# Hybrid mixer block on one core: the 31-tap convolution moved to the tensor engine and behind attention, projection weights split one block ahead

## The chip, the cores and the metric

One core of one Trainium2 chip runs the whole kernel. The metric is the time of one execution in microseconds of the device. TensorE (PE) multiplies matrices, VectorE (DVE), ScalarE (ACT) and GpSimd (POOL) work element by element, SyncE (SP) issues nearly all transfers. Each engine works off one queue in order.

## The reference

The model has two layers over 1024 latent tokens of width 1024 and 256 context tokens (`TL`, `TC`). A layer projects the normalised tokens once (`p = h @ w_in[l]`) and gives slices of `p` to four mixers of 256 channels each; a second projection and a mixture of 32 experts follow. The second layer has no outputs for the context, so most of its projections take the latent tokens alone. The mixers:

```python
y_a = rglru_mixer(...)       # 4-tap convolution u, gates r and i from u (64x64 blocks), linear scan, both directions, gated by gelu
y_b = diff_attn_mixer(...)   # differential attention
y_c = conformer_conv(...)    # below
y_d = hyena_mixer(...)       # 3-tap convolution, then twice: long convolution by Fourier transforms, times a gate

def conformer_conv(pc, conv_w, conv_b, ln_g, ln_b, w_pw, b_pw):
    u = pc[..., :W_C] * jax.nn.sigmoid(pc[..., W_C:])
    u = dwconv(u, conv_w, conv_b, (CONF_K // 2, CONF_K // 2))   # 31 taps, each channel for itself
    u = layer_norm(u, ln_g, ln_b)
    return jax.nn.silu(u) @ w_pw + b_pw
```

All of it is float32. The kernel keeps products exact to about that by splitting operands into a high and a low half of a reduced type (`fp32r`) and multiplying three times.

## The kernel before

Channels lie on the partitions, tokens along them, in pieces (`GROUPS`) of 512, 512 and 256 (context). The source is written in stages, and a scheduler orders each engine's queue when the program is built: what stands earlier in the source goes first where its inputs are expected to be ready. A buffer (`bufs`) that is still read holds up the next writer.

*Projections* (`phase1`, L2050). `win` (L1052) computes blocks of 128 columns of `w_in`. For every block it loads the weights (`wir`, one buffer), rounds them to `wih` on ScalarE and subtracts to `wil` on GpSimd (L959; two buffers each); then each piece takes 24 matmuls (L1073) into one PSUM bank and an evacuation. Block 0 and 1 feed the recurrence, 2 and 3 its output gates, 4 to 7 queries and keys, 10 to 13 the convolution mixer's GLU (12, 13 are the sigmoid halves), 14 to 19 hyena. `win_v` (L1101, matmuls L1115) makes the values. The order written is: block 0, recurrence 0, GLU blocks 12 and 10, GLU blocks 13 and 11, gate block 2, block 1, recurrence 1, then queries, keys and values, gate block 3.

`rglru` (L1385) goes through three steps of two directions: `rg_u` (4 taps: one GpSimd instruction L1410 and three on VectorE L1412, one buffer), two gate matmuls (L1415, into three PSUM banks `rg` shared by all), ScalarE functions to `rg_r`, `rg_i`, `rg_t` (two buffers each, released by the scan), products on GpSimd and VectorE and the scan (L1432, L1435).

`glu_evac` (L1119) leaves the GLU's output in `cu` in SBUF. `conv31` (L1452) is written behind all projections: 31 VectorE instructions for each of two channel blocks, each over all tokens at once,

```python
for j in range(1, 31):
    nc.vector.scalar_tensor_tensor(a, u[:, j:j + N], cw(j), a, op0=OP.mult, op1=OP.add)   # L1459
nc.sync.dma_start(self.cd[b * P:(b + 1) * P, :N], a)
```

*Attention* (L1161) follows, with the hyena blocks 14 to 19 of `win` between its matmuls (`rest`, L2113). In layer 0 it also has one part of the modulation for layer 1 (`modulation`, L962; matmuls L987 of two columns into four groups of 32 PSUM partitions), whose weights are loaded into the buffers `xa` and `cu` of the projections.

*Mixer stage* (L2183 to 2205). The order written is: `hyena_in` (L1721: load `hx`, three taps `hu` on GpSimd L1735 and VectorE L1738, transposes L1745) for blocks 0 and 1, hyena's first forward transform (`next(hy)`; matmuls L1782 with tables `tabc`), attention's output to channels, `hyena_in` for blocks 2 to 5, the whole `conformer` (L1472: load of `cd`, layer norm, pointwise product for every piece), the split of the output weights, and the rest of hyena. The output projection follows.

## Time and profile before

| | |
|---|---|
| median of three timed runs | 3564.89 us (3561.86 to 3567.80) |
| the profiled execution | 3568.25 us, of which the span of the trace is 3566.4 us |
| mean granted TensorE clock | 0.925 |
| TensorE busy | 3093.1 us (87%) |
| VectorE busy | 2296.5 us (64%) |
| ScalarE busy | 1538.4 us (43%) |
| GpSimd busy | 712.2 us (20%) |
| transfers | 743.33 MB, 208 GB/s on the mean |

Rows are read as follows. "L1459 DVE ... cacc<-cu,cw,cacc 128x1295 x120" is a group of 120 VectorE instructions of line 1459 that write `cacc`; behind the bar stand busy time in all, mean nanoseconds of one, and the idle time of the engine just before them with what ended it. In rows of a timeline the start comes first, then the duration, then the instruction; "x8" means eight instructions merged. PEclk is the clock that TensorE was granted as a share of full speed. A float32 matmul leaves two records, an `fp32r` one a single record. The recorded length of a matmul includes its run through the array, so its pace is read from the starts of neighbours.

### The profile page before, as it was taken

To read this page: it belongs to the slowest core of one execution; us is meant where nothing else is said; L and a number is where in the kernel's file an instruction comes from. 1 tells how busy PE (TensorE), PEld (TensorE's weight loads), DVE (VectorE), ACT (ScalarE), POOL (GpSimd) and SP (SyncE) were. 2 spreads that over 40 slices of the span, in tenths; PEclk is the share of its full clock that TensorE was granted. 3 is DMA by queue.
4 is the path that set the end of the run, shared out by engine and by line. 5 is a ranking of instruction groups with operands and counts; after the bars stand their busy time and mean duration, and the time that the engine had idled before them with its cause. 6 is when DMAs were issued, how large, how long until landed. Compare 5 with 4: busy or idle time off the path is not lost. (4 is left out here: it accounts for less than half of the span.)

```text
span 3566.4 us, 43889 instructions
## 1 busy us (share of the span) xinstructions
PE 3093.1 (87%) x14984; PEld 2083.0 (58%) x14984; DVE 2296.5 (64%) x3355; ACT 1538.4 (43%) x2497; POOL 712.2 (20%) x573
## 2 busy tenths in 40 slices
PE   5798788997899699999998587799788799899996
PEld 1246665775678354677555466667667665455563
DVE  6675885787768434476544779578876764357645
ACT  4234334772324233465543454367433343245523
POOL 2213451003210101111110445300330111111100
PEclk8899989998999699999999698889989899999998
DMA  5752226215455889987878512312446389978797
GB/s 184 232 193 62 72 88 213 72 38 191 159 194 189 269 305 321 360 312 240 316 252 324 198 33 101 135 34 70 160 150 217 135 297 369 386 278 282 263 348 297
DMA packets 415375, 743.33 MB, mean 208 GB/s; under 512 B 46219, under 2 KB 181240, under 8 KB 415146
## 3 DMA queue, kind: packets, MB, share of 16 engines
q1 hardware_dynamic: 397546, 702.69, 56.9%
q0 software_dynamic: 17600, 37.79, 3.1%
q8 instruction: 119, 1.95, 0.2%
q14 instruction: 110, 0.90, 0.1%
HBM read 656.13 MB, written 105.30 MB: 214 GB/s over the span
## 5 line engine op out<-in xcount | busy, mean ns | idle before, releaser
L679 DVE TENSOR_TENSOR wl<-wr,wh 128x1024 fp32r<-128x1024 f32 (+1 forms) x440 | 515.7, 1202 | 341.7 <-ACT wh L678 334.4
L678 ACT ACTIVATE wh<-wr 128x1024 fp32r<-128x1024 f32 (+1 forms) x440 | 442.5, 1038 | 381.8 <-PE mm L730 229.7
L734 PE MATMUL mm<-wr,xl 128*64 128x512 f32 x1216 | 327.9, 609 | 4.4 <-DVE xl L690 1.6
L1073 PE MATMUL mm<-hh,wih 128*128 128x512 f32 (+1 forms) x752 | 289.7, 386 | 12.1 <-ACT stg L1137 7.0
L1073 PE MATMUL mm<-hh,wil 128*128 128x512 f32 (+1 forms) x752 | 288.0, 384 | 10.7 <-POOL wil L959 9.9
L730 PE MATMUL mm<-wh,xh 128*128 128x512 f32 x704 | 289.5, 413 | 6.2 <-ACT wh L678 5.7
L1073 PE MATMUL mm<-hl,wih 128*128 128x512 f32 (+1 forms) x752 | 289.7, 385 | 1.4 <-DVE hl L959 0.8
L730 PE MATMUL mm<-wl,xh 128*128 128x512 f32 x704 | 278.7, 396 | 5.2 <-DVE wl L679 5.2
L730 PE MATMUL mm<-wh,xl 128*128 128x512 f32 x704 | 277.9, 396 | 0.0
L798 POOL DMA_INDIRECT fd<-ot,ridx x82 | 103.1, 1258 | 851.2 <-DVE ot L794 392.7
L1459 DVE SCALAR_TENSOR_TENSOR cacc<-cu,cw,cacc 128x1295 f32<-128x1295 f32 (+1 forms) x120 | 193.9, 1616 | 1.9
L671 POOL DMA_INDIRECT gb<-h2d,ridx x82 | 98.4, 1200 | 449.4 <-PE tr L698 197.1
L730 PEld LDWEIGHTS mm<-wh,xh 128*128 128x128 f32 x704 | 134.0, 190 | 92.0 <-issue 47.5
L1207 DVE TENSOR_REDUCE m<-A 128x1 f32<-128x1024 f32 x128 | 156.2, 1220 | 44.1 <-PE A L1197 36.1
L959 POOL TENSOR_TENSOR wil<-wir,wih 128x1024 fp32r<-128x1024 f32 x34 | 93.2, 2742 | 429.6 <-ACT wih L956 374.2
L734 PEld LDWEIGHTS mm<-wr,xl 128*64 128x64 f32 x1216 | 96.4, 137 | 140.8 <-issue 123.6
L1073 PEld LDWEIGHTS mm<-hh,wih 128*128 128x128 f32 x752 | 146.8, 196 | 42.5 <-ACT stg L1137 10.6
L1073 PEld LDWEIGHTS mm<-hh,wil 128*128 128x128 f32 x752 | 146.8, 195 | 39.2 <-POOL wil L959 11.5
L1073 PEld LDWEIGHTS mm<-hl,wih 128*128 128x128 f32 x752 | 147.0, 196 | 30.6 <-issue 6.3
L780 PE MATMUL mm<-wr,hl 128*64 128x512 f32 x608 | 154.6, 602 | 0.0
L730 PEld LDWEIGHTS mm<-wl,xh 128*128 128x128 f32 x704 | 134.1, 191 | 33.3 <-DVE wl L679 9.2
L1252 ACT ACTIVATE wT<-TR 128x512 f32<-128x512 f32 (+1 forms) x200 | 104.7, 524 | 108.3 <-PE TR L1247 99.0
(492 smaller groups left out, 6536.8 us busy)
## 6 DMA issues: line engine op xcount, KB each, us to landing
wr<-in_moe_w_gate_dram SPq DMA_DIRECT2D x256, 512.0 KB
wr<-in_moe_w_up_dram SPq DMA_DIRECT2D x256, 512.0 KB
wr<-in_moe_w_down_dram SPq DMA_DIRECT2D x256, 512.0 KB
wada<-in_w_ada_dram SPq DMA_DIRECT2D x48, 512.0 KB
tabc<-in_k_t_c_dram SPq DMA_DIRECT2D x88, 256.0 KB
wir<-in_w_in_dram SPq DMA_DIRECT2D x40, 512.0 KB
wr<-in_w_ada_dram SPq DMA_DIRECT2D x32, 512.0 KB
ks<-qkd SPq DMA_DIRECT2D x16, 640.0 KB
```

The source lines that it names most:

```text
L671: self.K.nc.gpsimd.indirect_dma_start(out=g[s, :D // (1 + h)], out_offset=None, in_=self.h2d[h], in_offset=bass.IndirectOffsetOnAxis(ap=id ...
L678: nc.scalar.activation(hi, src, AF.Copy)
L679: nc.vector.tensor_tensor(lo, src, hi.bitcast(FT), op=OP.subtract)
L730: nc.tensor.matmul(ps[b][w], x(k), y[:, kk], start=(k == 0 and c == 0), stop=(k == 7 and c == 2))
L734: nc.tensor.matmul(ps[b][0][w * 64:(w + 1) * 64], self.XT[n0 + b](k), raw[w][:, kk], start=(k == 0), stop=(k == 7))
L780: nc.tensor.matmul(po[b][0][o * 64:(o + 1) * 64], HT[b][:, k], raw[:, o], start=(k == 0), stop=(k == 3))
L798: s = nc.gpsimd.indirect_dma_start(out=self.fd[h], out_offset=bass.IndirectOffsetOnAxis(ap=ridx[r], axis=0), in_=ot[r], in_offset=None, bo ...
L959: (eng or nc.vector).tensor_tensor(lo, src, hi.bitcast(FT), op=OP.subtract)
L1073: nc.tensor.matmul(p[:, :n], a[:, k], b[:, k, t0:t0 + n], start=(k == 0 and a is wh and b is hh), stop=(k == 7 and a is wl))
L1207: nc.vector.tensor_reduce(m[:, c, 1:2], A[c], axis=AX.X, op=OP.max, negate=True)
L1252: nc.scalar.activation(o, i_, AF.Copy)
L1459: nc.vector.scalar_tensor_tensor(a, u[:, j:j + N], cw(j), a, op0=OP.mult, op1=OP.add)
```

## The change

The 31-tap convolution leaves VectorE. `glu_evac` writes the GLU's output to DRAM (`ud`). In the mixer stage `taps` arranges the weights as 64 diagonal matrices of 32 columns (`tapw`: channel in the columns, four taps times 32 channels along the rows), and `conv31` loads each piece of `ud` four times, shifted by one token each (`cr4`), so that one matmul does four taps of 32 channels; eight steps and four groups of 32 channels make a piece of 128 channels. `conformer` becomes a generator whose products and norms are called between hyena's steps; `hyena_in` for blocks 4 and 5 moves behind hyena's first inverse transform. In the projections, `rglru_conv` computes the six pieces of `rg_u` ahead of the GLU blocks (six buffers), the gate blocks move between queries and keys, `win` prepares the weights of the next block (`nxt`) with the low half on VectorE, and `stg` gets a third buffer. The modulation in layer 0's attention gets buffers of its own. The leftover experts, which run only under a condition read at run time, get a factor in layer 1.

```diff
+        self.ud = self.dram.tile([2 * P, UW], FT, name="ud")
+        z = c.tile([P, 2, 16], FT, name="zeros")
+        nc.vector.memset(z, 0.0)
+        for o, n in ((0, 15), (15 + TL, 15), (30 + T0, 16)):
+            nc.sync.dma_start(self.ud[:, o:o + n].rearrange("(b p) t -> p b t", p=P), z[:, :, :n])
...
+    def win_weights(self, l, w, ob, eng=None):
+        nc = self.nc
+        wl = w.tile([P, 8, P], FR, name="wil", bufs=2)
+        raw = w.tile([P, 8, P], FT, name="wir", bufs=1)
+        nc.sync.dma_start(raw, self.I["w_in"][l, :, ob * P:(ob + 1) * P].rearrange("(k p) f -> p k f", p=P))
+        wh = w.tile([P, 8, P], FR, name="wih", bufs=2)
+        self.split(raw, wh, wl, eng=eng or nc.gpsimd)
+        return wh, wl
...
+        W = [self.ready.pop(ob, None) or self.win_weights(l, w, ob, eng) for ob in obs]
+        if nxt is not None and len(obs) == 1:
+            self.ready[nxt] = self.win_weights(l, w, nxt, nc.vector)
...
+                if nxt is not None and nxt not in self.ready and t0 == groups[-1][0] and len(obs) == 2:
+                    self.ready[nxt] = self.win_weights(l, w, nxt, nc.vector)
                 evac(p, t0, n, v)
...
         def g(p, t0, n, v):
             o = t0 + 15 + (15 if v else 0)
-            nc.vector.scalar_tensor_tensor(u[:, o:o + n], th[0][:, :n], 1.0, p[:, :n], op0=OP.add, op1=OP.mult)
+            t = th[0][:, :n]
+            nc.vector.scalar_tensor_tensor(t, t, 1.0, p[:, :n], op0=OP.add, op1=OP.mult)
+            nc.sync.dma_start(self.ud[b * P:(b + 1) * P, o:o + n], t)
...
+    def rglru_conv(self, l, w, b, xa):
+        nc, res = self.nc, []
+        for s in range(3):
+            for d in range(2):
...
+                u = w.tile([P, 512], FT, name="rg_u", bufs=6)[:, :n]
+                nc.gpsimd.tensor_scalar(u, xa[:, o:o + n], cw(0), self.pc("a_conv_b", d * 2 + b), op0=OP.mult,
+                                        op1=OP.add)
+                for j in range(1, 4):
+                    nc.vector.scalar_tensor_tensor(u, xa[:, o + j:o + j + n], cw(j), u, op0=OP.mult, op1=OP.add)
+                res.append(u)
...
+    def taps(self, l, w):
+        R = w.tile([64, 4, 32], FT, name="taps", bufs=1)
+        nc.gpsimd.memset(R, 0.0)
+        for j in range(8):
+            m = min(4, 31 - 4 * j)
+            nc.sync.dma_start(R[j * 8:(j + 1) * 8, :m],
+                              bass.AP(tensor=cw.tensor, offset=cw.offset + 4 * j * 256, ap=[[32, 8], [256, m], [1, 32]]))
+        p = self.pr.tile([P, 512], FT, name="rg")
+        nc.tensor.transpose(p[:, :64], R.rearrange("r s c -> r (s c)"), self.ident[:64, :64])
+        t = w.tile([P, 64], FT, name="tapsT", bufs=1)
+        nc.scalar.activation(t, p[:, :64], AF.Copy, scale=0.5)
...
+        W = w.tile([P, 64, 32], FT, name="tapw", bufs=1)
+        nc.gpsimd.tensor_tensor(W, one[:, None, :].to_broadcast([P, 64, 32]), t[:, :, None].to_broadcast([P, 64, 32]),
+                                op=OP.mult)
...
+    def conv31(self, w, b, W, out, t0, n):
+        x = w.tile([P, 4, 540], FT, name="cr4", bufs=2)
+        u = self.ud[b * P:(b + 1) * P].rearrange("(g c) t -> c g t", g=4)
+        o = t0 + (15 if t0 >= TL else 0)
+        for s in range(4):
+            nc.sync.dma_start(x[s * 32:(s + 1) * 32, :, :n + 28], u[:, :, o + s:o + s + n + 28])
+        p = self.pr.tile([P, 512], FT, name="rg")
+        for j in range(8):
+            for g in range(4):
+                nc.tensor.matmul(p[g * 32:(g + 1) * 32, :n], W[:, j * 8 + b * 4 + g], x[:, g, 4 * j:4 * j + n],
+                                 start=(j == 0), stop=(j == 7))
+        nc.scalar.activation(out, p[:, :n], AF.Identity, bias=self.pc("c_conv_b", b))
...
+        for t0, n, _ in GROUPS[:3 if ctx_out else 2]:
+            accs.append(w.tile([P, 2, 512], FT, name="cx", bufs=3))
             for b in range(2):
-                nc.sync.dma_start(acc[:, b, :n], self.cd[b * P:(b + 1) * P, o:o + n])
+                self.conv31(w, b, W, accs[-1][:, b, :n], t0, n)
+            yield
+        for (t0, n, _), acc in zip(GROUPS, accs):
...
-                    h = recur(0)
                     for b in range(2):
-                        u = wd.tile([P, N], FT, name="cu", bufs=2)
...
+                        if b:
+                            xa, f = self.rglru_in(xap)
+                            self.win(l, w, [b], hs, GROUPS, [f], nxt=13)
+                            xs.append(xa)
+                        us = self.rglru_conv(l, rg, b, xs[b])
+                        self.win(l, w, [12 + b, 10 + b], hs, allg, self.glu_evac(wd, b),
+                                 nxt=4 if b else 1)
+                        hs_.append(self.rglru(l, rg, b, us, prm, ctx_out))
...
                         for i in range(2):
-                            self.win(l, w, [4 + i], hs, allg, [self.qk_evac(wq, 0, i, rope)])
-                            self.win(l, w, [6 + i], hs, GROUPS, [self.qk_evac(wq, 1, i, rope)])
+                            self.win(l, w, [4 + i], hs, allg, [self.qk_evac(wq, 0, i, rope)],
+                                     nxt=6 + i)
+                            self.win(l, w, [6 + i], hs, GROUPS, [self.qk_evac(wq, 1, i, rope)], nxt=2 + i)
                             if i == 0:
                                 self.win_v(l, w, wq, hs, vt)
-                        gate(1, h)
-                for b in range(2):
-                    self.conv31(l, wd, b, us[b], ctx_out)
+                            gate(i, hs_[i])
...
+                cv = self.pool(c2, "cv")
...
-                        [lambda: wd.tile([P, N], FT, name="cu", bufs=2)] * 2
+                        [lambda: cv.tile([P, D], FT, name="cu", bufs=2)] * 2
...
+                    cm = self.conformer(l, w, ctx_out, self.taps(l, w))
                     for b in range(2):
                         self.hyena_in(l, hc, b, ut, ctx_out)
+                    next(cm)
                     next(hy)
+                    next(cm)
                     self.to_channels(w, yt, 1, nblk)
-                    for b in range(2, 6):
+                    if ctx_out:
+                        next(cm)
+                    for b in range(2, 4):
                         self.hyena_in(l, hc, b, ut, ctx_out)
-                    self.conformer(l, w, ctx_out)
+                    next(cm)
+                    next(hy)
+                    for b in range(4, 6):
+                        self.hyena_in(l, hc, b, ut, ctx_out)
+                    for _ in cm:
+                        pass
+                    next(hy)
```

## Rows read from the trace of the kernel before

**Rows 1.** Stages: length; busy PE, PEld, DVE, ACT, POOL; PEclk, DMA share, GB/s

```profile
294.00:554.00 260.00, 213.54 (x1072) 174.24 (x1071) 201.38 (x178) 105.47 (x142) 120.87 (x74) 0.91 0.25 81
576.00:832.00 256.00, 239.68 (x1723) 170.73 (x1721) 202.48 (x357) 177.58 (x439) 11.82 (x10) 0.98 0.24 78
832.00:842.00 10.00, 0.02 (x1) 0.05 (x1) 4.31 (x3) 0.00 (x0) 3.47 (x4) 0.62 0.92 303
842.00:1016.00 174.00, 139.93 (x597) 112.09 (x598) 135.08 (x172) 48.86 (x73) 65.08 (x68) 0.88 0.55 180
2057.00:2294.00 237.00, 194.97 (x894) 154.26 (x892) 187.10 (x176) 102.05 (x135) 114.01 (x72) 0.90 0.23 77
2533.00:2700.00 167.00, 128.07 (x537) 100.95 (x532) 131.92 (x167) 43.09 (x64) 60.73 (x62) 0.86 0.53 167
```

**Rows 2.** Waits of TensorE in projections, layer 0, then 1: total, times, longest

```profile
PE rg L1415 <- DVE rg_u L1412: 37.4, 11, 6.4
PE mm L1073 <- POOL wil L959: 8.2, 1, 8.2
...
PE rg L1415 <- DVE rg_u L1412: 39.2, 10, 7.5
PE rg L1415 <- POOL wil L959: 2.4, 1, 2.4
```

**Rows 3.** Groups of instructions: the 31-tap convolution

```profile
L1459 DVE SCALAR_TENSOR_TENSOR cacc<-cu,cw,cacc 128x1295 f32<-128x1295 f32 (+1 forms) x120 | 193.9, 1616 | 1.9
```

**Rows 4.** Timeline of TensorE, projection matmuls: start, duration, instruction

```profile
555.22 0.39 PE L1073 MATMUL mm<-hh,wil 128*128 128x512 f32 x1
...
558.16 0.39 PE L1073 MATMUL mm<-hh,wih 128*128 128x512 f32 x1
```

**Rows 5.** Busy time of single lines: L1073 in both layers, L1115, L1415

```profile
294.00:554.00 260.00, 162.19 (x784) 134.17 (x783) 0.91 0.25 81
2057.00:2294.00 237.00, 142.54 (x606) 113.50 (x604) 0.90 0.23 77
...
294.00:554.00 260.00, 30.65 (x240) 29.48 (x240) 0.91 0.25 81
...
294.00:554.00 260.00, 29.28 (x48) 10.73 (x48) 0.91 0.25 81
```

**Rows 6.** Timeline of TensorE: unsplit, 64-wide and four-group matmuls

```profile
913.62 3.70 PE L1506 MATMUL rg<-cx,wpw 128*128 128x512 f32 x8
...
1699.89 3.65 PE L780 MATMUL mm<-wr,hl 128*64 128x512 f32 x16
...
150.73 1.13 PE L1642 MATMUL mm<-f_x,tab 128*128 128x512 f32 x2
151.79 0.61 PE L987 MATMUL mp<-wada,sT 128*2 128x256 f32 x8
152.33 1.12 PE L1642 MATMUL mm<-f_x,tab 128*128 128x512 f32 x2
```

**Rows 7.** Timeline of VectorE: one weight split

```profile
276.35 1.22 DVE L959 TENSOR_TENSOR wil<-wir,wih 128x1024 fp32r<-128x1024 f32 x1
```

**Rows 8.** Groups of instructions: weight split on GpSimd, hyena's input

```profile
L959 POOL TENSOR_TENSOR wil<-wir,wih 128x1024 fp32r<-128x1024 f32 x34 | 93.2, 2742 | 429.6 <-ACT wih L956 374.2 <-PE mm L1073 33.5 <-PE A L1197 22.0
...
L1738 DVE SCALAR_TENSOR_TENSOR hu<-hx,pp,hu 128x1281 f32<-128x1281 f32 (+1 forms) x24 | 42.5, 1773 | 10.7 <-POOL hu L1735 10.5
```

**Rows 9.** Timeline of SP, VectorE and TensorE where layer 0's mixer stage starts

```profile
831.54 0.32 SPq L1728 DMA_DIRECT2D hx<-pd  x1
...
832.38 0.42 SPq L1730 DMA_DIRECT2D hx<-pd  x1
...
837.65 7.23 DVE L1738 SCALAR_TENSOR_TENSOR hu<-hx,pp,hu 128x1281 f32<-128x1281 f32 x4 [5.88 <-POOL hu L1735]
...
850.19 1.56 PE L1782 MATMUL mm<-z_x,tabc 128*128 128x256 f32 x6 [0.19 <-DVE z_x L1693]
```

**Rows 10.** Timeline of SP: first weight load of the second modulation

```profile
522.06 0.43 SPq L984 DMA_DIRECT2D cu<-in_w_ada_dram  x1
```

102 lines of the change are left out of this document (40 added, 62 removed).

## The prediction

> **What bounds the kernel now.** I read the profile page first (TensorE busy 87% of the span, VectorE 64%), then the busy time of every engine stage by stage [rows 1], then who TensorE waited for in the stages that the change touches [rows 2], and last single rows for prices. In rows 1 the reader is to see three kinds of stretch. Attention (576 to 832 us) keeps TensorE busy 239.7 of 256 us at a clock of 0.98; nothing the change does can be worth much there. The projection stage (294 to 554 us in layer 0, 2057 to 2294 us in layer 1) keeps it busy only 213.5 of 260 and 195.0 of 237 us, at 0.91 and 0.90, while VectorE is at 201.4 and 187.1. The mixer stage behind attention (842 to 1016, 2533 to 2700) is busy 139.9 of 174 and 128.1 of 167 us at 0.88 and 0.86, behind 10 us in layer 0 (832 to 842) with hardly anything on TensorE.
>
> The 46.5 us that TensorE stands idle in layer 0's projections are nearly all named: 37.4 us for `rg_u`, the 4-tap convolution in front of the recurrence's gate matmuls, and 8.2 us for a weight half `wil` that GpSimd splits. In layer 1 it is 39.2 and 2.4 of 42.0 us [rows 2]. TensorE works its queue off in order, so projections that were ready stood behind those gate matmuls. The 31-tap convolution (120 instructions, 193.9 us, half in each layer) fills VectorE in just this stage [rows 3].
>
> **What the projections would cost without stalls.** A 128x512 projection matmul follows the last one every 0.226 us (13 steps from 555.22 to 558.16) [rows 4]; a 256-wide one takes 30.65/240 = 0.128 us [rows 5]. A weight block of 24 matmuls a piece costs 24 x (2 x 0.226 + 0.128) = 13.9 us over three pieces, 10.9 over the two latent ones. Layer 0 has 11 blocks here (784 records against 11 x 72 = 792), layer 1 three of three pieces and eight of two (606 against 600) [rows 5]. The values take 30.7 us; the gates are 48 records, 32 of them 512 wide at 3.70/8 = 0.46 us and 16 half as wide [rows 5, 6]: 18.5 us. That is 153 + 31 + 18 = 202 us in layer 0 and 129 + 31 + 18 = 178 in layer 1. Both stretches are 58 to 59 us longer than that: 46.5 and 42 idle, the rest slow clock.
>
> **The change, part by part.**
>
> *VectorE loses the 31 taps*, some 97 us a layer. It gains nine weight splits a layer (blocks 12, 1, 13, 4, 6, 2, 5, 7, 3) at 1.22 us [rows 7] = 11 us that GpSimd had at 2.74 us each [rows 8]. It keeps about 201 - 97 + 11 = 115 us in a stage of some 215: it no longer sets the pace.
>
> *The 4 taps run one step ahead*, with six buffers for `rg_u` in place of one, and the GLU projections (two blocks, 28 us) are queued between them and the gates. `rg_u` is then ready when a gate matmul comes up, and the 37.4 and 39.2 us go. *Weights split a block ahead*: a block lasts 10.9 us or more, and the wait of 8.2 (2.4) goes. What is late next is the gates' three PSUM banks: ScalarE can't drain them before `rg_r`, `rg_i` and `rg_t` (two buffers each) are released by the scans. No row shows that wait, since `rg_u` is later today; its bounds are 0 and today's 38 a layer. I take 10 a layer, nearer zero, because 28 us (22 in layer 1) of GLU matmuls and then the second block's queue lie between. Of the slow clock (12 and 17 us) I give back half, since the stretches at full clock, as 0.98 in attention, are those without stalls. Layer 0: -46 + 10 - 6 = -42. Layer 1: -42 + 10 - 8 = -40. Sum **-82 us**.
>
> New on SP's queue here are six (four) writes of `ud`, each waiting for its VectorE product, with the next weight load and the `qkd` writes behind it. The weights are a block early, so that is hidden; without this cover it would be a microsecond or two each.
>
> *The products on TensorE.* A piece of 512 columns of one channel block is 8 steps of 4 matmuls into four 32-wide column groups, 64 records. The nearest row is the modulation's matmul, 2 columns wide in the same four groups: eight 256-wide records from 151.79 to 152.33, 0.0675 us each [rows 6]; so 0.135 at 512, and 64 x 0.135 = 8.6 us a piece. Layer 0 has the worth of five pieces, layer 1 of four: 43 + 35 = 78 us. Below stands 0.46/4 = 0.116 (67 us in all); above, the 64-wide pair with two groups at 3.65/16 = 0.228 (131 us), and no overlap at 0.46 (266 us). I take 78, whose row has four groups, as here.
>
> How much of it is covered? The mixer stage at full clock holds 139.9 x 0.88 = 123 us of TensorE work in 174, and 128.1 x 0.86 = 110 in 167. With the products that is 166 and 145. At attention's yield (239.7 x 0.98/256 = 0.92) they need 181 and 158 us: there is nearly room, if the order fits. It does not all fit. The tap loads (eight small ones, 0.32 to 0.42 us on SP as the `hx` loads) come ahead of `hx`, 3 us, and GpSimd's `tapw` product, 2048 wide, takes about 2 x 2.74 = 5.5 us [rows 8, 9], of which I count half ahead of hyena's own GpSimd step, which starts the chain `hx` at 831.54, `hu` at 837.65, first transform at 850.19 [rows 9]. That is **+6** a layer (0 to 10). Two pieces of products, 17 us, are queued ahead of that transform; the gap they could fill is 10 us plus the 6, but their inputs pass through the same late taps and 2.2 MB of `cr4` loads in a stretch at 303 GB/s already [rows 1]. I let half show: **+8** a layer (0 to 17). The second pair and the context pieces fall into hyena's wait for its own products. Against this, hyena's inputs 4 and 5 and two of the three norms now stand behind its first inverse transform: two times two `hu` steps at 1.77 us [rows 8] leave a full VectorE: **-5** a layer (0 to -10). Sum +9 a layer, **+18**.
>
> By the Trainium skill ("TensorEngine Tiling (Array Packing)", Key Properties) a change of the array's tiling mode drains TensorE. The rows agree: two unsplit records between such batches take 1.06 us (150.73 to 151.79) where 0.92 would do [rows 6]. If each of the 80 steps alternated with an unsplit matmul, that would add 80 x 0.14 = 11 us and give 3516.
>
> *Modulation in layer 0's attention.* Its weights went into the convolution's old buffers from 522 us on [rows 10]; now into a pool of their own, free only when the projections end. Its 128 records (8.6 us at the price above) then fill the first stalls of attention less well, and 8 MB of loads meet the first `qs` loads: **+4** (0 to 9). The lines about the leftover experts stand under a condition and I cost them at nothing; three small `ud` writes at the start lie beside other loads.
>
> **Sum.** -82 + 18 + 4 = -60. The profiled execution takes 3568.25 us (its span plus 1.85), 3.4 above the median of 3564.89; the difference is taken over to the median: **3505 us**.
>
> **The rivals.**
>
> *Stalls vanish wholly, products fit.* Both projection stages reach their 202 and 178 us (-117) and the mixer stage loses only the late start and the modulation's share, about 10: 3458. For it: the idle time is nearly all named. Against: attention, with no such chain, still loses 16 of 256 us.
>
> *The gate matmuls wait for the drain instead.* Three quarters of the 38 us a layer come back as waits for PSUM, as the two-buffered `rg_r` chain is as long as before: the gain shrinks to about 34, less 22: 3553. Against: the six buffers and the GLU block in between.
>
> *Products uncovered (slower).* In the mixer stage TensorE is in order, and hyena's transforms stand behind the products. If each piece lands on the chain, its whole 78 us show, plus 12 for late starts and 4: -82 + 94 = +12, 3577. It decides once more than some 60 of the 78 are exposed without the -5 a layer. Against it: 34 and 39 us of idle time in the stage.
>
> *Column groups don't overlap.* At 0.46 us a record the products are 266 us; idle time and slow clock cover about 130, so +136, +16 for the rest, -82: 3635. The row at 0.0675 speaks against it.
>
> **How the numbers follow.** Chances: forecast 0.60 (its own range 3480 to 3530), everything fits 0.15, drain 0.12, uncovered 0.08, no overlap 0.05. A measurement of this kernel tells 0.2%, 7 us, from no change. The first two and three quarters of the third are faster: 0.84. The rest of the third and the mildest of the fourth are within 0.2%: 0.05. What is left is slower: 0.11. From 3448 to 3552 the range holds the first, nearly all of the second and a good half of the third.
>
> **What would show it.** Right: no wait of TensorE for `rg_u` in the projections and stretches of about 218 and 197 us at a clock over 0.95; VectorE near 115 us there; records of the products at 0.13 us; the mixer stages some 10 us longer. Wrong: waits of the gate matmuls for ScalarE over 15 us a layer; a product piece over 12 us; a first hyena transform more than 20 us after the last projection plus today's gap.

## The result and the profile after

The changed kernel takes **3581.6 us** (median of 14 runs, 3573.4 to 3587.7), the kernel before 3561.3 beside it. The ratio is 1.0052, with a 95% interval of 1.0042 to 1.0063: 15 to 22 us slower, where 60 us faster was forecast. The profiled execution has a span of 3578.0 us; TensorE is busy 3122.1 us (3093.1 before), VectorE 2112.2 (2296.5). So VectorE lost 184 us and TensorE got 29 more (69 us of products, less what its other work gained). TensorE is idle for 456 us of the span, where it was for 473: nearly all the idle time is still there.

Stages of the changed kernel, as in rows 1 (length; busy PE, PEld, DVE, ACT, POOL; PEclk, DMA share, GB/s): projections, attention, the gap behind it and the mixer stage of layer 0, then projections and mixer stage of layer 1.

```profile
280.00:554.00 274.00, 237.13 (x1226) 197.84 (x1224) 109.58 (x139) 101.03 (x147) 91.45 (x73) 0.93 0.31 101
555.00:791.00 236.00, 221.63 (x1640) 158.46 (x1639) 188.31 (x335) 169.03 (x421) 11.56 (x4) 0.99 0.26 83
791.00:825.00 34.00, 16.34 (x88) 12.26 (x89) 20.53 (x26) 8.55 (x19) 8.21 (x13) 0.81 0.44 112
825.00:1034.00 209.00, 177.73 (x978) 123.36 (x978) 130.55 (x171) 52.19 (x79) 56.89 (x65) 0.90 0.54 167
2013.00:2306.00 293.00, 233.24 (x1114) 189.59 (x1114) 134.35 (x172) 118.47 (x181) 110.25 (x82) 0.89 0.30 101
2531.00:2709.00 178.00, 144.49 (x748) 100.50 (x747) 127.99 (x159) 43.88 (x63) 56.65 (x63) 0.87 0.56 163
```

Against [rows 1] VectorE is down from some 200 to 110 us in layer 0's projections, but TensorE's clock there is 0.93 and not over 0.95. The mixer stage has 38 us more of TensorE (139.9 to 177.7) and is 35 us longer (174 to 209), at the same share of busy time.

All kernels are compared below by four lengths from the timelines of their profiled executions. **P0, P1**: from the first projection matmul to the first of attention, in layers 0 and 1. **M0**: from attention's last matmul to the first expert matmul in layer 0, **M1**: from attention's last to the first matmul of the router (`lg`, L1991) in layer 1, which starts some 27 us into the output projection. Attention's last matmul is the last one on the values (`PO<-wT,vt`); the projection matmuls of hyena's blocks run some 11 us past it.

| kernel | median us | ratio to before (95%) | P0 | P1 | M0 | M1 |
|---|---|---|---|---|---|---|
| before | 3561.3 | 1 | 300 | 308 | 415 | 187 |
| **changed** | 3581.6 | 1.0052 (1.0042, 1.0063) | 274 | 293 | 457 | 210 |
| e1_weights | 3551.3 | 0.9972 (0.9959, 0.9985) | 262 | 269 | 460 | 211 |
| e3_hyfirst | 3585.1 | 1.0073 (1.0052, 1.0094) | 273 | 289 | 458 | 212 |
| e4_noprod | (see text) | | 275 | 289 | 439 | 192 |
| e6_oldproj | 3575.2 | 1.0034 (1.0020, 1.0047) | 274 | 281 | 459 | 210 |
| e7_cr3 | 3538.2 | 0.9935 (0.9915, 0.9954) | 261 | 269 | 454 | 211 |
| e8_order | 3544.0 | 0.9945 (0.9926, 0.9964) | 262 | 269 | 455 | 211 |
| e9_half | 3552.9 | 0.9975 (0.9963, 0.9987) | 278 | 277 | 437 | 208 |
| e10_actq | 3524.3 | 0.9888 (0.9869, 0.9907) | 242 | 260 | 452 | 213 |
| e11_behind | 3516.1 | 0.9870 (0.9849, 0.9891) | 243 | 258 | 455 | 213 |
| e12_twice | 3626.4 | 1.0179 (1.0160, 1.0199) | 275 | 290 | 479 | 234 |
| e13_crtwice | 3514.2 | 0.9865 (0.9836, 0.9895) | 245 | 258 | 452 | 214 |
| e14_half | 3501.6 | 0.9846 (0.9818, 0.9874) | 255 | 268 | 427 | 199 |
| e15_orderonly | 3557.5 | 0.9980 (0.9966, 0.9994) | 300 | 308 | 404 | 190 |
| e16_oldorder | 3511.8 | 0.9835 (0.9815, 0.9855) | 255 | 269 | 432 | 208 |
| e17_along | 3594.9 | 1.0094 (1.0072, 1.0116) | 303 | 309 | 441 | 194 |
| e18_alongq | 3610.5 | 1.0140 (1.0114, 1.0166) | 303 | 305 | 443 | 199 |
| e19_alonglate | 3577.1 | 1.0045 (1.0032, 1.0059) | 303 | 308 | 430 | 189 |
| **e20_halflate** | 3488.7 | 0.9806 (0.9782, 0.9829) | 256 | 269 | 416 | 190 |

So the change gained 26 and 15 us in the projections (forecast 42 and 40) and lost 41 and 23 in the mixer stages (forecast 9 and 9). That is 23 us slower; the 12 us by which the profiled spans differ are that, less 11 of small shifts elsewhere, attention among them. Attention's own length hardly changed (245 to 243 us, 220 to 220).

**The new waits in the projections.** TensorE's waits in these stretches, layer 0 and then layer 1 (total us, times, longest), as [rows 2] of before:

```profile
PE mm L1132 <- ACT wvh L965: 16.7, 2, 10.3
PE mm L1088 <- POOL wil L968: 10.0, 1, 10.0
PE mm L1132 <- POOL wvl L968: 3.4, 2, 2.1
PE mm L1088 <- ACT wih L965: 3.1, 1, 3.1
...
PE rg L1447 <- ACT rg_i L1448: 0.6, 2, 0.3
...
PE mm L1132 <- ACT wvh L965: 15.7, 2, 13.8
PE mm L1088 <- POOL wil L968: 11.0, 2, 8.0
```

No line names `rg_u` any more, and ScalarE's drain is short, so that part went as forecast. The waits are for weights. L1132 are the values, whose weights nobody split ahead; `wil` on POOL is the second block of a GLU pair, which was not split ahead either. GpSimd's timeline shows why the latter became late (start, us, instruction):

```profile
356.08 5.41 POOL L1416 TENSOR_SCALAR rg_u<-xa,pp 128x256 f32<-128x256 f32 x4
361.45 3.04 POOL L1470 TENSOR_TENSOR h<-h,h 128x1280 f32<-128x1280 f32 x1
364.48 3.12 POOL L1416 TENSOR_SCALAR rg_u<-xa,pp 128x512 f32<-128x512 f32 x2
367.57 2.76 POOL L968 TENSOR_TENSOR wil<-wir,wih 128x1024 fp32r<-128x1024 f32 x1
...
370.39 0.79 PE L1088 MATMUL mm<-hh,wil 128*128 128x512 f32 x1 [9.98 <-POOL wil L968]
```

The six first taps, now issued together, stand ahead of the split. For the values the two loads go through the single buffer `wir`, which gate block 2's weights hold until VectorE has split them (the first line below, 3.49 us in place of 1.22 in [rows 7]); only then SP loads, ScalarE rounds and TensorE goes on:

```profile
428.84 3.49 DVE L968 TENSOR_TENSOR wil<-wir,wih 128x1024 fp32r<-128x1024 f32 x1
...
432.36 0.37 SPq L1125 DMA_DIRECT2D wir<-in_w_in_dram  x1
...
438.01 1.05 ACT L965 ACTIVATE wvh<-wir 128x1024 fp32r<-128x1024 f32 x1
...
439.11 1.23 PE L1132 MATMUL mm<-wvh,hh 128*128 128x256 f32 x4 [10.30 <-ACT wvh L965]
```

**The mixer stage.** The group of the products (line, shapes, count | busy us, mean ns of one | idle before), then TensorE between hyena's first forward and first inverse transform in layer 0, then SP in the same stretch, then the start of the same inverse in the kernel before:

```profile
L1520 PE MATMUL rg<-cr,tapw 128*32 128x512 f32 (+1 forms) x640 | 68.9, 579 | 9.4 <-DMA cr<-ud 8.2 <-ACT tch L1369 1.2
```

```profile
830.17 15.21 PE L1520 MATMUL rg<-cr,tapw 128*32 128x512 f32 x128
845.31 1.13 PE L1849 MATMUL mm<-z_x,tabc 128*128 128x256 f32 x4
...
871.01 1.91 PE L1520 MATMUL rg<-cr,tapw 128*32 128x512 f32 x2 [4.71 <-DMA cr<-ud]
872.85 3.78 PE L1849 MATMUL mm<-ut,tab 128*128 128x256 f32 x8
876.57 14.20 PE L1520 MATMUL rg<-cr,tapw 128*32 128x512 f32 x126
890.70 2.50 PE L1363 MATMUL rg<-ident,yt 128*128 128x128 f32 x20
895.30 1.97 PE L1849 MATMUL mm<-Yl,tabc 128*128 128x256 f32 x8 [2.10 <-DMA tabc<-in_k_t_c_dram]
```

```profile
867.07 0.38 SPq L1739 DMA_DIRECT2D tab<-in_k_t_s_dram  x1
867.49 19.31 SPq L1516 DMA_DIRECT2D cr<-ud  x8
886.85 0.43 SPq L1795 DMA_DIRECT2D hx<-pd  x1
...
888.75 0.43 SPq L1739 DMA_DIRECT2D tabc<-in_k_t_c_dram  x1
```

```profile
892.82 1.06 PE L1782 MATMUL mm<-Yl,tabc 128*128 128x256 f32 x2
```

The inverse (the matmuls on `Yl`) begins 50 us after the forward transform (845.3 to 895.3); before it was 42.6 (850.2, [rows 9], to 892.8). A run of 126 products stands ahead of it, and in SP's queue its table and the next `hx` stand behind eight `cr` loads that take 19.3 us, because a `cr4` buffer comes free only when a product piece has read it. The forward transform itself begins 48 us after attention's last matmul, where it began after 30.

Part of the late start lies on VectorE. Its four steps of `hu` for blocks 0 and 1 take 10.59 us, where they took 7.23 [rows 9]: the first of them begins beside GpSimd's `tapw` product.

```profile
817.08 3.63 POOL L1504 TENSOR_TENSOR tapw<-tap,tapsT 128x2048 f32<-128x2048 f32 x1
817.14 10.59 DVE L1805 SCALAR_TENSOR_TENSOR hu<-hx,pp,hu 128x1281 f32<-128x1281 f32 x4 [7.76 <-POOL hu L1802]
```

### The profile page after: what moved, and what is told of

It is laid out like the page before. It is cut to its first block, busy times and chain, and to the rows that moved or that the text cites. A ratio compares the mean times of both kernels' runs of the same rounds, so it can differ in the third digit from the quotient of the medians.

```text
span 3578.0 us, 45179 instructions
## 1 busy us (share of the span) xinstructions
PE 3122.1 (87%) x15626; PEld 2077.3 (58%) x15626; DVE 2112.2 (59%) x3250; ACT 1516.5 (42%) x2489; POOL 632.6 (18%) x549
## 5 line engine op out<-in xcount | busy, mean ns | idle before, releaser
L733 PEld LDWEIGHTS mm<-wh,xl 128*128 128x128 f32 x704 | 133.6, 190 | 28.8
L1241 ACT ACTIVATE E<-A,m 128x1024 f32<-128x1024 f32 x128 | 143.1, 1118 | 0.0
```

Source lines behind the costliest of these rows:

```text
L733: nc.tensor.matmul(ps[b][w], x(k), y[:, kk], start=(k == 0 and c == 0), stop=(k == 7 and c == 2))
L1241: nc.scalar.activation(e[:, :TL], A[c], AF.Exp, bias=m[:, c, 2:3], accum_out=s[:, c, 1:2])
```

## The experiments

**Is it the weights?** e1 prepares the two late weights ahead:

```diff
+                        self.ready[10 + b] = self.win_weights(l, w, 10 + b, nc.vector)
                         us = self.rglru_conv(l, rg, b, xs[b])
...
+                        wv = self.win_v_weights(l, w, wq)     # loads and splits of win_v, ahead of block 4
                         for i in range(2):
```

> The changed kernel, with the two weight waits of its projections taken away: the second GLU block's weights (10, 11) are loaded and split on VectorE ahead of the 4 taps, and the value weights are loaded and split ahead of block 4 instead of behind block 6. In the changed kernel TensorE waits 10.0 us for `wil` on GpSimd and 23.2 us for `wvh`, `wvl` and `wih` in layer 0, and some 33 us for the same in layer 1. Theory (these waits ate the projections' gain): both go, the projection stretches fall from 274 and 293 us by 15 to 25 us each, and the time is 30 to 50 us below the changed kernel's 3582, at 3530 to 3550. Rival (the waits only cover others, ScalarE's and the recurrence's, which come up instead): the stretches fall by less than 5 us each, 3572 to 3582.

P0 fell by 12 us (15 to 25 were expected) and P1 by 24, the time by 30, to just under the kernel before. The theory holds in the main, with its time a hair above the range. In layer 0 a wait of 14.0 us was left: the two halves of the value weights now held `wir` when block 6 wanted it.

**What did the projections' reordering bring?** e6 undoes it and keeps the rest:

```diff
-                        us = self.rglru_conv(l, rg, b, xs[b])
-                        self.win(l, w, [12 + b, 10 + b], ..., nxt=4 if b else 1)
+                    h = recur(0)          # taps inside each step, one rg_u buffer
+                    for b in range(2):
+                        self.win(l, w, [12 + b, 10 + b], hs, allg, self.glu_evac(wd, b))
+                    gate(0, h)
+                    h = recur(1)
```

> The mixer part of the change alone: products on TensorE behind attention as in the changed kernel, but the projections in the old order with the old recurrence (one buffer for `rg_u`, taps inside each step, weights split on GpSimd, nothing split ahead); the 31 taps are off VectorE. Theory A (the 4 taps waited because of the 31 taps around them on VectorE): with VectorE empty the wait for `rg_u` falls to under 20 us a layer without any reordering, and the time is within 10 us of the changed kernel: 3572 to 3592. Theory B (the reordering itself made the 26 and 15 us): they come back, and the time is 3615 to 3625, some 55 to 65 us over the kernel before.

The time is within 10 us of the changed kernel and rather below it. So an empty VectorE is enough for what the projections gained; the reordering, with its two late weights, gave nothing in layer 0 and cost 12 us in layer 1. Theory A holds in its time, not in its wait: `rg_u` still cost 29.3 and 23.4 us. The granted clock does not follow the idle time alone: in layer 0 e6 has 35 us of it in P0, the longest wait 4.9 us, at a clock of 0.96, the changed kernel 38 us, the longest 10.3, at 0.93.

**How much of the products shows?** e4 leaves seven of eight steps out, e12 does all twice:

```diff
-        for j in range(8):
+        for j in range(1):                 # e4
+        for j in list(range(8)) * 2:       # e12
```

> The changed kernel, with seven of the eight steps of every product piece left out (one of eight remains, so the convolution is not computed; loads, tap preparation and evacuation stay). It leaves out 560 of 640 product records, 60 us of TensorE by their own busy time of 68.9 us. Theory (the products are uncovered): the time falls by 50 to 60 us, to 3522 to 3532, 35 us of it in layer 0's mixer stage and 22 in layer 1's. Rival (the products are half covered and the late start, the loads and the moved norms cost the rest): it falls by 20 to 35 us, to 3547 to 3562.

> The changed kernel with every product step computed twice into the same PSUM bank (the second pass starts the sum anew), so that the output is the same and TensorE has 640 more records, 69 us by the busy time of the first 640; loads, order and everything else stay. Theory A (a product shows with its whole length, since TensorE is the stage's bound by then): 60 to 70 us more, 3642 to 3652. Theory B (half of it falls into waits, as where seven eighths were left out): 30 to 40 us more, 3612 to 3622.

Without the sums the router sees other values and the experts take other rows, so e4's whole time (3671.7 us) says nothing; its stages up to the router do. M0 and M1 are 18 us shorter each, for 35 and 25 us of products. Doubling costs 1.27% of the time, 45 us (37 to 53, the half widths of the two intervals added as squares), for 61 us of products by their busy time (130.0 us in e12, 68.9 in the changed kernel). It fell between the theories: some two thirds to three quarters of a product show. And even without them M0 is 23 us over the kernel before: the products are not the whole loss.

**Does their place matter?** e3 writes the first transform ahead of the first products; e8, on e1 with three `cr4` buffers, writes all but two pieces behind the first inverse transform, with hyena_in of blocks 2 to 5 ahead of it.

```diff
                     for b in range(2):
                         self.hyena_in(l, hc, b, ut, ctx_out)
+                    cm = self.conformer(l, w, ctx_out, self.taps(l, w))
-                    next(cm)
                     next(hy)
                     next(cm)
+                    next(cm)
```

> The changed kernel, with the tap loads and the tap product written behind hyena_in of blocks 0 and 1, and hyena's first forward transform ahead of the first two pieces of products. Theory (order: the late first transform delays the whole chain of the mixer stage): the first transform in layer 0 starts 15 to 20 us after the first hyena transpose's old place allows, that is 13 us earlier against the end of attention than the 54 us of the changed kernel, the stage of layer 0 ends 10 to 20 us earlier and that of layer 1 about 10, together 20 to 30 us: 3552 to 3562. Rival (total: TensorE and VectorE take turns through the whole stage, so the products show wherever they stand): the first transform is earlier but the output projection starts within 5 us of before in each layer, 3574 to 3584.

> The kernel of the mended weight waits, three buffers for `cr4`, and another order in the mixer stage: hyena_in of blocks 0 and 1, first forward transform, attention's output to channels, tap preparation, hyena_in of blocks 2 to 5, the first two pieces, first inverse transform, then all other pieces and the norms, second forward transform. So only 15 us of products stand ahead of the inverse, and the others come while VectorE works between the inverse and the second forward transform, where TensorE stood idle 6 of 24 us in the kernel before. Theory (what counts is which gap of TensorE the products fall into): the mixer stages end 10 to 20 us earlier than with three buffers alone, both together, 3522 to 3538. Rival (products are exposed by their total, wherever they stand): within 4 us of the three-buffer kernel.

e3's forward transform starts 33.5 us after attention in place of 47.9, and M0 and M1 end no earlier: the rival's outcome. e8 is no faster than e7, the same with the changed kernel's order (6 us over it by the medians, 4 by the ratios). Both only moved the gap. In e8 the four hyena_in pieces and 15.5 us of products stood between forward and inverse transform instead.

**The buffer and the queue.** e7 is e1 with a third `cr4` buffer; e10 adds ScalarE's queue for those loads, and the value weights ahead of the second GLU pair; e11 puts the tap preparation behind the first hyena_in, its loads on ScalarE's queue too.

```diff
-        x = w.tile([P, 4, 540], FT, name="cr4", bufs=2)
+        x = w.tile([P, 4, 540], FT, name="cr4", bufs=3)
-            nc.sync.dma_start(x[s * 32:(s + 1) * 32, :, :n + 28], ...)
+            nc.scalar.dma_start(x[s * 32:(s + 1) * 32, :, :n + 28], ...)
...
+                        if b:
+                            wv = self.win_v_weights(l, w, wq)
                         self.win(l, w, [12 + b, 10 + b], ...)
```

> The kernel of the mended weight waits (3551.3), with three buffers for `cr4` in place of two. In the changed kernel SP stands 20.5 us in layer 0's mixer stage waiting for a `cr4` buffer that a product piece still reads, with the loads of `hx` for blocks 2 and 3 and of a table `tabc` queued behind it; VectorE then waits 15.2 us in one piece for the `hu` made of that `hx`, and the first inverse transform starts 50 us after the first forward one, where the kernel before took 43. Theory (the buffer wait in SP's queue holds up the chain): the inverse starts 5 to 12 us earlier in layer 0, and the time falls to 3539 to 3547. Rival (TensorE has the products to do in that gap anyway, 14 us in one piece ahead of the inverse): under 3 us, 3548 to 3554.

> The kernel with mended weight waits and three buffers for `cr4` (3538), with two more waits taken away, each readable in its own stage. Projections: the value weights are loaded and split ahead of the second GLU block's matmuls, a block earlier than before, so that block 6's load no longer stands behind them for the one buffer `wir` (TensorE waited 14.2 and 3.8 us for it in layer 0). Mixer stage: the `cr4` loads are issued from ScalarE's queue, so that SP's queue (`hx`, tables) never stands behind a `cr4` buffer; SP still stood 10.0 us for one in layer 0. Theory: the projections get 10 to 18 us shorter in layer 0 and 3 to 8 in layer 1, the mixer stage 3 to 8 us in layer 0; 3512 to 3526. Rival (in the projections the recurrence's gates come up in place of the weights, and in the mixer stage TensorE has its products to do at that place anyway): under 6 us in all, 3532 to 3540.

> The same kernel with the tap preparation written behind hyena_in of blocks 0 and 1 instead of ahead, and its eight loads on ScalarE's queue. In the changed kernel the first hyena transpose in layer 0 starts 27.4 us after attention's last matmul, 21.9 in the kernel before. Theory (late start as priced, 6 us a layer): the first transpose comes 5 us earlier in layer 0, and the time falls by 3 to 8 us against the kernel without it. Rival (the stage is held by TensorE's total and by the tables further on): the start is earlier, the end within 2 us.

e7 gained 13 us by its median and 6 in M0, but not as its theory had it: SP's wait for a `cr4` buffer fell from 20.5 to 10.0 us, and the inverse still started 60 us after the forward transform, where it was 51 in e1 (5 to 12 earlier were expected). e10's gain lies in the projections: P0 fell by 19 and P1 by 9 us, and with the weights really ahead nothing long is left of TensorE's waits (e10, layer 0's projections, first three lines; in layer 1 the longest at a gate is 6.4 us, for ScalarE's `rg_r`):

```profile
PE mm L1088 <- ACT wih L965: 3.1, 1, 3.1
PE mm L1088 <- DVE wil L968: 2.2, 2, 1.6
PE rg L1451 <- ACT rg_r L1452: 1.8, 1, 1.8
```

```profile
281.00:522.00 241.00, 230.51 (x1224) 192.48 (x1222) 110.43 (x141) 99.47 (x145) 89.15 (x71) 0.98 0.35 115
```

The granted clock there is 0.98 (0.93 in the changed kernel, 0.91 before). M0 and M1 together did not move with the queue, so half of e10's theory fell. e11 starts the first hyena transpose 20.9 us after attention (25.7 in e10) and its time is lower by 8, within both intervals; M0 did not follow. There the `tapw` product stands beside VectorE's first sums for the transform, and one of these takes 4.12 us in place of 0.69.

**Is it the bytes?** e13 moves every `cr4` load's bytes a second time, to a place that nobody reads:

```diff
+        for s in range(4):
+            z = self.dram.tile([P, 540], FT, name=...)
+            nc.scalar.dma_start(z[:, :n + 28], self.ud[b * P:(b + 1) * P, o + s:o + s + n + 28])
```

> The best kernel so far (3516), with the bytes of every `cr4` load moved a second time: four more transfers a piece from `ud` to scratch memory that nobody reads, of the same size (128 rows of 2.2 KB), issued from ScalarE's queue behind the real ones. The output is the same. With seven eighths of the products left out, layer 0's stage from attention's end to the experts was still 23 us longer than in the kernel before, and TensorE waited 28 us there for loads (`tab`, `cr4`, `tabc`) where it had waited 7. Theory (the 5.5 MB of `cr4` loads in layer 0 take transfer time from the tables, some 25 us at 200 to 250 GB/s): the doubled loads lengthen layer 0's stage by 15 to 25 us and layer 1's by 5 to 15, 3536 to 3556. Rival (the transfers have room; what is left is the order): under 6 us in all, 3512 to 3522.

10 MB more (751.1 to 761.1) cost nothing that shows: the ratios put it 2 us below e11, give or take 13. The transfers have room for them; the rival holds.

**The order alone, and the company alone.** e15 gives the kernel before the new order of norms and hyena_in; e16 takes that order from e14 (below).

```diff
-                    for b in range(2, 6):
+                    for b in range(2, 4):
                         self.hyena_in(l, hc, b, ut, ctx_out)
-                    self.conformer(l, w, ctx_out)
+                    next(cm)
+                    next(hy)
+                    for b in range(4, 6):
+                        self.hyena_in(l, hc, b, ut, ctx_out)
+                    for _ in cm:
+                        pass
+                    next(hy)
```

> The kernel before with one part of the change alone: the order of the mixer stage as in the changed kernel (loads of the convolution's result by piece, hyena_in of blocks 2 and 3, the norm of the first piece, first inverse transform, hyena_in of blocks 4 and 5, the other norms, second forward transform); the 31 taps stay on VectorE in the projections, there are no products. In the forecast the deferred hyena_in and norms were worth 5 us a layer of gain. With seven eighths of the products left out, layer 0's stage from attention's end to the experts was 438.5 us against 415.4 of the kernel before. Theory A (the order makes most of these 23 us): layer 0's stage is 10 to 20 us longer than in the kernel before, 3570 to 3585. Theory B (the order costs nothing, it is what comes along with the products: their loads' place, tap preparation, evacuations): within 4 us, 3556 to 3568. The forecast's -5 a layer: 3550 to 3556.

> The best kernel so far (3501.6, half of the channels' taps as products), with the order of the kernel before in the mixer stage: hyena_in of blocks 0 and 1, first forward transform, to channels, hyena_in of blocks 2 to 5, then products and norms whole, then the rest of hyena. Theory A (the new order costs 10 to 20 us in layer 0): 3482 to 3494. Theory B (order is worth nothing by itself): 3497 to 3507. Theory C (the new order gains the forecast's 5 us a layer): 3508 to 3514.

The order alone gains 7 us (2 to 12), and M0 is 11 us shorter: theory A fell, and the forecast's 10 us stand inside the interval. e16's median is 10 us over e14's and its stages 14, but its ratio is not higher: it says nothing against that and settles nothing.

e17 adds to e15 all that the products bring with them, and one of their eight steps, into a buffer that nobody reads. e18 is the same with e11's three changes, e19 with the second and the context group behind the inverse transform (the first norm goes there with them):

```diff
                     next(hy)
-                    next(cm)
                     self.to_channels(w, yt, 1, nblk)
-                    if ctx_out:
-                        next(cm)
                     for b in range(2, 4):
                         self.hyena_in(l, hc, b, ut, ctx_out)
-                    next(cm)
                     next(hy)
+                    next(cm)
+                    if ctx_out:
+                        next(cm)
```

> The kernel before with the order of the mixer stage (3557) and, beside it, all that comes along with the products but seven eighths of the products themselves: GLU output also written to `ud`, tap preparation ahead of hyena's first input, `cr4` loads on SP's queue with two buffers, one of eight steps (80 records, 9 us of TensorE) and an evacuation of every piece on ScalarE. Their result goes to a buffer that nobody reads; the convolution itself still comes from VectorE in the projections, so the output is the same. Theory A (what comes along costs the 28 us that neither products nor order explain): 3575 to 3590. Theory B (little of it shows without the products; products and their company delay each other): under 10 us more than 3557, 3555 to 3567.

> As the run before, with what the best kernels changed of it: three buffers for `cr4`, its loads and those of the taps on ScalarE's queue, the tap preparation behind hyena_in of blocks 0 and 1. If theory A holds because of SP's queue and the late start, this one is 10 to 20 us faster than that; if the cost lies in the engines' work (evacuations, tap product, the 80 records), within 4 us of it.

> The kernel before with the order and all that comes along with the products (3595), with the second group and the context group written behind hyena's first inverse transform, and hyena_in of blocks 2 and 3 ahead of it. In the run before it layer 0's forward transform ended at 891 us and the inverse began at 919; between stood three product pieces, each waiting 6.3 us for its `cr4` load, on TensorE's queue, and `hx` and the inverse's `tabc` behind those loads in SP's queue. Theory (this round of load, product, freed buffer, next load ahead of the inverse is the company's cost): the gap in layer 0 falls from 28 to under 8 us and the time by 18 to 30 us, to 3565 to 3577. Rival (the gap is only moved behind the inverse): under 6 us, 3589 to 3595.

The company costs 1.14%, 41 us (31 to 50) against e15, with an eighth of the products; M0 is 37 us longer. (e17 also still loads the convolution's result from `cd` between the `cr4` loads, which the changed kernel does not.) The first fence is e17's TensorE between the two transforms, the second e19's:

```profile
887.43 3.57 PE L1831 MATMUL mm<-ut,tab 128*128 128x256 f32 x8 [4.87 <-DMA tab<-in_k_t_s_dram]
890.93 1.06 PE L1500 MATMUL rg<-cr,tapw 128*32 128x512 f32 x8
898.28 1.94 PE L1500 MATMUL rg<-cr,tapw 128*32 128x512 f32 x8 [6.29 <-DMA cr<-ud]
900.15 4.43 PE L1346 MATMUL rg<-ident,yt 128*128 128x128 f32 x20
906.42 0.64 PE L1500 MATMUL rg<-cr,tapw 128*32 128x256 f32 x8 [1.84 <-DMA yd<-tch]
913.35 1.08 PE L1500 MATMUL rg<-cr,tapw 128*32 128x256 f32 x8 [6.29 <-DMA cr<-ud]
918.95 2.05 PE L1831 MATMUL mm<-Yl,tabc 128*128 128x256 f32 x4 [4.52 <-DMA tabc<-in_k_t_c_dram]
```

```profile
899.67 3.75 PE L1831 MATMUL mm<-ut,tab 128*128 128x256 f32 x8 [5.04 <-DVE Yl L1866]
903.21 0.94 PE L1794 MATMUL rg<-ident,hu 128*128 128x128 f32 x4
903.99 0.60 PE L1831 MATMUL mm<-Yl,tabc 128*128 128x256 f32 x2
```

In e17 TensorE does 5 us of products in 28, between the forward transform's end (891) and the inverse (919): two of its four pieces wait 6.3 us each for a load that could start only when an earlier piece had freed its buffer. In e19 the inverse follows within 1 us, and 18 us of the 41 are gone, just at the weak end of what was expected. e18 shows that another queue and one more buffer are no remedy: from the forward to the inverse transform it takes 46 us in place of 58, but M0 is no shorter, and the time is 16 us (4 to 28) over e17's.

**The best kernel.** e9 and e14 put block 0's taps back on VectorE, on e8 and on e11; e20 is e14 with e19's order.

```diff
+                self.conv31d(l, xap, 0, cu, ctx_out)          # 31 taps on VectorE, behind the projections
...
-            for b in range(2):
-                self.conv31(w, b, W, accs[-1][:, b, :n], t0, n)
+            nc.sync.dma_start(accs[-1][:, 0, :n], self.cd[:, o:o + n])
+            self.conv31(w, 1, W, accs[-1][:, 1, :n], t0, n)
```

> The kernel of the other order, with the 31 taps of channel block 0 back on VectorE behind the projections (31 instructions a layer, some 48 us; its GLU output stays in the core's memory, the accumulator lies in the buffer `xa`, `rg_u` has four buffers), and only block 1 as products: 320 of 640 records, 34 us of TensorE. Theory (products cost TensorE's time in the mixer stage by about half their length, 18 us of 34 and 18 of 26 where seven eighths were left out, while VectorE has 150 us free in a projection stage): the mixer stages get 15 to 20 us shorter in all, the projections no longer, 3505 to 3525. Rival (VectorE's taps bring the waits for `rg_u` back or run into attention): the projections and attention lose 10 us or more a layer and the time is no lower than with the other order alone.

> The best kernel so far (3516), with the 31 taps of channel block 0 back on VectorE behind the projections and block 1 alone as products (half of the records, 34 us of TensorE, and half of the `cr4` loads). Products twice cost 45 us for 69. Theory (two thirds of a product's length show; VectorE has 150 us free in a projection stage, and the value weights no longer wait for the buffer): the mixer stages get 20 to 25 us shorter in all, the projections and attention at most 8 longer: 3496 to 3506. Rival (the taps on VectorE cost the projections and attention what the products cost the mixer stage, as in the run with half the products before, where the projections took 16 and 8 us more): 3512 to 3525.

> The best kernel so far (3501.6, half of the channels' taps as products), with its second and context group behind the first inverse transform in the same way. Theory: with three buffers and loads on ScalarE's queue less of the gap is left, 5 to 12 us off, 3489 to 3497. Rival (nothing left to win there, or the norms come later than the second forward transform can bear): 3498 to 3508.

In e9 the mixer stages fell by 18 and 3 us as the theory had it, and the projections rose by 16 and 8, as the rival had it, so that the time is 9 us over e8's. In e14 the projections still rose by 12 and 10, more than the 8 allowed, the mixer stages fell by 29 and 14, and the median by 15 (0.9870 to 0.9846 by the ratios, 9 us). e20's median is 13 us below that (by the ratios 14, give or take 13), and at 0.9806 (0.9782 to 0.9829) it is faster than the kernel before by 61 to 78 us. M0 and M1 are back at what they were before the change, 416 and 190.

## Why the prediction was wrong

*VectorE loses the taps*: right, 201 to 110 us with 115 forecast. The taps were not half and half, but 103.9 us in layer 0 and 90.0 in layer 1, which makes the forecast 108.

*The 4 taps a step ahead*: the wait for `rg_u` went as said, and ScalarE's drain, taken at 10 us a layer, was 0.6 and 4.0. The step ahead itself is worth less than the sum: e6, in the old order, gains 27 us a layer from the empty VectorE.

*"Weights split a block ahead: the wait goes"*: **this step failed**. I let every weight be a block early. The change passes one block as `nxt`; the second block of each GLU pair and the values are not in it. I had listed the nine splits myself and did not ask which were missing, nor what the six taps on GpSimd and the one buffer `wir` put in front of these. They cost 33 us of waits in layer 0 and as much in layer 1, and part of the clock with them (0.93 in layer 0, 0.98 where they are mended). With them mended, e10 has P0 242 and P1 260, that is 58 and 48 less than before, where the forecast had 42 and 40. So that sum was too low for what the idea is worth, and 41 too high for what was written.

*Price of a product*: right. 68.9 us for 640 records against 78; a piece of 64 records took 7.6 us (15.21 for two) against 8.6, and 7.2 at the higher clock of a later run (14.20 for 126 records). Four column groups do overlap.

*How much is covered*: **this step failed too**. I found room from the stage's total, 0.92 of its length, and let 16 us of 78 show. Two thirds to three quarters show (e4, e12). The room was there as an average, but the stage is a chain (forward transform, VectorE, inverse, VectorE, forward), and its idle times lie where the products' inputs or the order don't let them go.

*What comes along*: the late start was right in layer 0 (27.4 us to the first transpose against 21.9; 6 forecast) and nothing in layer 1. The `tapw` product's share of it is right in size, but it was paid on VectorE (3.4 us of `hu`) more than on GpSimd. Not priced at all were the two queues between the transforms, SP's and TensorE's: I had counted the loads' bytes and not the round of load, product and freed buffer, with `hx` and `tabc` behind it. By the stages alone the sum closes: M0 and M1 together are 603 us in the kernel before, 594 in e15, 631 in e4 and 667 in the changed kernel. That is -9 for the order, +37 for the company with an eighth of the products, and +36 for the other seven eighths, 64 in all where 18 was forecast. Of the company, 18 us of e17's 41 are shown to hang on where the pieces stand (e19).

*Order, -5 a layer*: right (-7 for both, 2 to 12). *Modulation, +4*: nothing, attention is 2 us shorter.

*The array's mode*: by the Trainium skill ("TensorEngine Tiling (Array Packing)", Key Properties) a change drains. The trace agrees, and it is cheap: the last four products of the first run start at 844.78 and the transform's first matmul at 845.31, 0.53 us later, where fours of products follow each other every 0.45 (14.13 us for 126). The +11 for alternating steps did not come up, as the scheduler kept the products in runs of 126 or 128 records, but for one of two; no run here has the steps alternating.

*The rivals*: "products uncovered" gave 3577 and comes nearest, but not by its sum: it had -82 in the projections and +94 behind, where -41 and +64 happened. Its point of decision, 60 of the products' 78 us exposed, was not reached; the projections' halved gain and the company made up for it.

*The signs*: none of the signs of being wrong came up. ScalarE's waits and the price of a piece stayed small, and the first transform stands 36.7 us after the last projection matmul, 19.0 before, just inside the 20 allowed. They watched the terms that I had priced; the late weights and the loads' place in the queues had no sign of their own.

**What stays open.** After e19's order 23 us of the company's 41 remain, and no run splits them by cause: evacuations, tap preparation and the norms' later end are all in it. By place, M0 of e19 is 26 us longer than in e15; 5 of these come ahead of the first transpose, and 15 or 16 behind hyena's last inverse matmul, from where it took 240 us to the first expert in e19, 232 in e17 and 224 in e15. Why e18 is slower than e17 is open as well: their profiled executions differ by 4 us only, and the four lengths by 3 in sum. That SP's queue and not TensorE's holds up the inverse is not shown apart: e7 and e18 eased SP's, and M0 fell by 6 us in the one and not at all in the other.

## What to carry to other kernels

When a change prepares things ahead, list what is *not* prepared, and what the prepared ones now hold: a single buffer or an engine's queue turns the rest later than it was. Idle time summed over a stage is no room for new work; ask at which places of its chain the engine is idle, whether the new work's inputs are there by then, and what its own loads stand in front of. Doubling the new work, leaving most of it out, and adding its company without it to the old kernel price the two apart.

## What the hardware showed that I had not expected

Four 32-column groups ran at 0.119 us a 512-wide record (15.21 us for 128, at a granted clock of 0.91) and 0.113 (14.20 for 126, at 0.98), about a quarter of the 0.46 us of the unsplit one [rows 6]. 10 MB more of transfers in the mixer stages, issued from ScalarE's queue, cost nothing that shows (3514.2 against 3516.1 us).

The weight split on VectorE that took 3.49 us (428.84 to 432.33, above) began while GpSimd was adding `h`, and ended 1.1 us after GpSimd had:

```profile
428.36 2.89 POOL L1470 TENSOR_TENSOR h<-h,h 128x1280 f32<-128x1280 f32 x1 [1.40 <-DVE h L1467]
```

The Trainium skill ("SBUF — State Buffer", SBUF: two separate sides) says that a VectorE operation with two inputs from SBUF and a GpSimd one that reads SBUF take a common pair of ports in turn, each for the whole instruction. This row agrees: GpSimd ended at 431.25, which makes 2.4 us of waiting and then 1.1 us, about the 1.22 of [rows 7]. The `hu` beside the `tapw` product, above, agrees too.
